# Trace of a matrix product: from casting loads on the software queue to plain float32 loads on SyncE's hardware queue, two rows to a partition

## The chip, the cores and the metric

The kernel runs on one core of a Trainium2 chip. The metric is device time in microseconds (us), lower is better. A run lasts some 740 us, and the spread of the kernel before is 0.03% (737.23 to 737.42 us).

The DMA figures are for the sixteen DMA engines that serve the core. "GB/s" in a slice of a profile counts the bytes written. A load that rounds float32 to bf16 on its way writes half of what it reads, so for such loads the rate of reading is twice the figure shown.

## The reference

```python
B, N = 8, 2176
a, b = randn(B, N, N), randn(B, N, N)          # float32
prod = np.matmul(a, b)
traces = np.diagonal(prod, axis1=1, axis2=2).sum(axis=-1)   # 8 numbers
```

The trace of A·B is the sum over all i and j of A[i,j]·B[j,i]. No matrix product is needed: transpose B, multiply with A element by element, and add up. Each number of A and B is used once, so 2 × 8 × 2176² × 4 bytes = 303 MB have to come from HBM, the memory that holds the inputs, and little is computed on them.

## The kernel before

A of one batch is 17 blocks of 128 rows, B too. All loads go through GpSimd's software queue and are rounded to bf16 on the way. TensorE transposes 128 × 128 blocks of B into PSUM, the memory that takes its results, and one VectorE instruction multiplies 512 columns with A and adds them up.

```python
KGW = 4
a_pool = tile_pool(bufs=2 * NT); b_pool = tile_pool(bufs=2 * KGW); psum_pool = tile_pool(bufs=7)
for bi in range(BATCH):
    for j_blk in range(NT):                        # all of A of this batch
        a_tile = a_pool.tile([P, N], bf16)
        nc.gpsimd.dma_start(out=a_tile, in_=a[bi, j_blk * P:(j_blk + 1) * P, :])
    for kg in range(N_KG):                         # groups of four blocks of B
        for kc in range(kc_lo, kc_hi):
            b_tile = b_pool.tile([P, N], bf16)
            nc.gpsimd.dma_start(out=b_tile, in_=b[bi, kc * P:(kc + 1) * P, :])
        for j_blk in range(NT):
            # up to 4 transposes of b_chunks[i][:, j_blk block] into psum_tile [P, 512] bf16
            # tensor_tensor_reduce(a_tiles[j_blk][:, kc_lo*P:kc_hi*P] * psum_tile) -> acc column
    # ... (sum of acc into one column per batch; at the end one small matmul sums the partitions)
```

Of the kernel before, what the change touches and what calls it, by code (L numbers as in the profile page):

```python
# [1 line left out]

# [6 lines left out]


@with_exitstack
def kernel(
    ctx: ExitStack,
    tc: tile.TileContext,
    a: bass.AP,
    b: bass.AP,
    out: bass.AP,
):
    nc = tc.nc  # L20
    P = 128
    BATCH, N, N2 = a.shape
    assert N == N2
    assert N % P == 0
    NT = N // P

    KGW = 4
    F = KGW * P
    N_KG = (NT + KGW - 1) // KGW

    dt = mybir.dt.bfloat16

    const = ctx.enter_context(tc.tile_pool(name="const", bufs=1))
    identity = const.tile([P, P], dt, tag="identity")
    make_identity(nc, identity)
    ones = const.tile([P, 1], mybir.dt.float32, tag="ones")
    nc.vector.memset(ones, 1.0)  # L37
    batch_accs = const.tile([P, BATCH], mybir.dt.float32, tag="batch_accs")
    result_tile = const.tile([P, BATCH], mybir.dt.float32, tag="result")

    a_pool = ctx.enter_context(tc.tile_pool(name="a_pool", bufs=2 * NT))
    b_pool = ctx.enter_context(tc.tile_pool(name="b_pool", bufs=2 * KGW))
    psum_pool = ctx.enter_context(tc.tile_pool(name="psum", bufs=7, space=bass.MemoryType.PSUM))
    psum_small = ctx.enter_context(tc.tile_pool(name="psum_small", bufs=1, space=bass.MemoryType.PSUM))
    scratch_pool = ctx.enter_context(tc.tile_pool(name="scratch", bufs=4))
    acc_pool = ctx.enter_context(tc.tile_pool(name="acc", bufs=2))

    for bi in range(BATCH):
        a_tiles = []
        for j_blk in range(NT):  # L50
            a_tile = a_pool.tile([P, N], dt, tag="a")
            nc.gpsimd.dma_start(out=a_tile, in_=a[bi, j_blk * P:(j_blk + 1) * P, :])  # L52
            a_tiles.append(a_tile)

        acc = acc_pool.tile([P, NT * N_KG], mybir.dt.float32, tag="acc")

        for kg in range(N_KG):
            kc_lo = kg * KGW
            kc_hi = min(kc_lo + KGW, NT)
            gw = kc_hi - kc_lo  # L60
            fw = gw * P

            b_chunks = []
            for kc in range(kc_lo, kc_hi):
                b_tile = b_pool.tile([P, N], dt, tag="b")
                nc.gpsimd.dma_start(out=b_tile, in_=b[bi, kc * P:(kc + 1) * P, :])  # L66
                b_chunks.append(b_tile)

            for j_blk in range(NT):
                psum_tile = psum_pool.tile([P, F], dt, tag="bT")  # L70
                for i, b_tile in enumerate(b_chunks):
                    nc.tensor.transpose(  # L72
                        psum_tile[:, i * P:(i + 1) * P],
                        b_tile[:, j_blk * P:(j_blk + 1) * P],
                        identity,
                    )
                scratch = scratch_pool.tile([P, F], dt, tag="scr")
                nc.vector.tensor_tensor_reduce(  # L78
                    out=scratch[:, :fw],
                    in0=a_tiles[j_blk][:, kc_lo * P:kc_hi * P],  # L80
                    in1=psum_tile[:, :fw],
                    scale=1.0,
                    scalar=0.0,
                    op0=mybir.AluOpType.mult,
                    op1=mybir.AluOpType.add,
                    accum_out=acc[:, j_blk * N_KG + kg: j_blk * N_KG + kg + 1],
                )

        nc.vector.reduce_sum(  # L89
            out=batch_accs[:, bi:bi + 1], in_=acc, axis=mybir.AxisListType.X  # L90
        )

    batch_psum = psum_small.tile([1, BATCH], mybir.dt.float32, tag="bp")
    nc.tensor.matmul(batch_psum, ones, batch_accs, start=True, stop=True)  # L94
    nc.vector.tensor_copy(out=result_tile[:1, :BATCH], in_=batch_psum)  # L95

    nc.sync.dma_start(
        out=out.rearrange("(a b) -> a b", a=1),
        in_=result_tile[:1, :BATCH],
    )  # L100


# [1 line left out]
_INS = ['a', 'b']  # L104
_OUTS = [((8,), 'float32')]


# [23 lines left out]
```

## Time and profile before

| | before |
|---|---|
| time, median | 737.3 us |
| read from HBM | 303 MB |
| read rate in full slices | 2 × 214 = 428 GB/s |
| VectorE / TensorE busy | 50% / 37% |
| after the chain's last wait for a load | 17 us |

These are lines of the page of before: busy time of the engines (PE is TensorE, PEld its weight loads, DVE VectorE, ACT ScalarE, POOL GpSimd), the GB/s moved in each of 40 slices of 18.4 us, the queue that all loads use, and the shares of the chain that ended last.

```profile
PE 271.7 (37%) x2314; PEld 217.7 (30%) x2314; DVE 364.8 (50%) x1370; POOL 144.4 (20%) x278
GB/s 175 213 214 215 213 215 213 214 214 214 214 213 214 214 214 214 213 214 213 214 214 213 214 213 214 214 213 215 213 214 214 213 214 214 214 214 213 161 209 29
q0 software_dynamic: 39168, 151.54, 102.2%
HBM read 303.04 MB, written 0.00 MB: 412 GB/s over the span
DMA 80%; issue 16%; POOL 1%; DVE 1%; PE 0%; POOLq 0%; DVEq 0%
```

The queue's packets took 102% of sixteen engines' span (overlapping packets count twice), every slice but the first and the last few stands at 213 to 215 GB/s, and no other engine is near its limit. The loads bound the kernel. The exceptions at the end are 161 and then 29.

The chain of waits of before, near its end (start in us, duration in us, what):

```profile
705.64 12.94 DMA b_tile<-in_b_dram
718.63 0.30 PE psum_tile L72
...
732.96 0.25 DVE batch_accs L89
733.25 0.21 PE batch_psum L94 x2
```

The last wait for a load ends at 718.6 us and the span at 735.6. In between VectorE works off what it could not start earlier, because a group of four blocks of B must have landed before the first of its reductions can run. That is the tail of 17 us. (The very last block of B lands at 721.2 us by the trace, 14.4 us before the end, but its turn comes after the others.)

These are two groups of the same profile, by line and shape: engine, operation, shapes, count, busy time and the mean ns of one.

```profile
L78 DVE CUSTOM_DVE_ANT_0 scratch<-a_tile,psum_tile 128x512 bf16<-128x512 bf16 x544 | 333.5, 682 | 364.3 <-PE psum_tile L72 364.1
L72 PE MATMUL psum_tile<-identity,b_tile 128*128 128x128 bf16 x2312 | 271.5, 286 | 460.3 <-DMA b_tile<-in_b_dram 434.1 <-DVE acc L78 22.4
```

Both engines' idle time is released by the engine before them, and in the end by the loads.

### The profile page before, as it was taken

The page shows a single profiled execution, that of the slowest core. Times are in us where ns is not written, and L with a number is a line of the kernel's source. Part 1 is how long each engine was busy: PE and PEld are TensorE (multiplying, and loading weights), DVE is VectorE, ACT ScalarE, POOL GpSimd, SP SyncE. Part 2 cuts the span into 40 slices and gives each one's busy share as a digit, 9 for nine tenths or more (in the row PEclk, how much of TensorE's full clock was granted, in tenths as well). Part 3 has the DMA queues.
Part 4 walks back from the last instruction along what each step waited for, and adds up shares of the span by engine and source line. Part 5 has one row for each costly group of instructions (what it writes and reads, how often), then busy time and mean ns, then how long its engine had stood idle before and what let it go on. Part 6 is the DMA issues. An engine that isn't in the chain of part 4 may idle for free.

```text
span 735.6 us, 7232 instructions
## 1 busy us (share of the span) xinstructions
PE 271.7 (37%) x2314; PEld 217.7 (30%) x2314; DVE 364.8 (50%) x1370; POOL 144.4 (20%) x278
## 2 busy tenths in 40 slices
PE   0016441174412744035450453505453054520665
PEld 0005430163301533024340343403342034410454
DVE  0007673087610967019570285704766056750698
POOL 4221221112121221212222122221222222221110
PEclk9999775557655556556655556555556556665575
DMA  8999999999999999999999999999999999999891
GB/s 175 213 214 215 213 215 213 214 214 214 214 213 214 214 214 214 213 214 213 214 214 213 214 213 214 214 213 215 213 214 214 213 214 214 214 214 213 161 209 29
DMA packets 39208, 152.00 MB, mean 207 GB/s; under 512 B 4354, under 2 KB 4354, under 8 KB 39170
## 3 DMA queue, kind: packets, MB, share of 16 engines
q0 software_dynamic: 39168, 151.54, 102.2%
q8 instruction: 18, 0.29, 0.1%
q14 instruction: 20, 0.16, 0.1%
q1 hardware_dynamic: 2, 0.00, 0.0%
HBM read 303.04 MB, written 0.00 MB: 412 GB/s over the span
## 4 chain that ended last, share of the span: by engine, by line
DMA 80%; issue 16%; POOL 1%; DVE 1%; PE 0%; POOLq 0%; DVEq 0%
DMA b_tile<-in_b_dram 51%; DMA a_tile<-in_a_dram 29%; POOL b_tile L66 1%; DVE scratch L78 1%; DVE acc L78 1%; POOL a_tile L52 0%; PE psum_tile L72 0%; POOLq L66 0%; POOL identity masks.py:199 0%; DVE batch_accs L89 0%; PE batch_psum L94 0%; DVEq L78 0%; POOL identity masks.py:197 0%; DVE result_tile L95 0%; POOLq masks.py:199 0%
## 5 line engine op out<-in xcount | busy, mean ns | idle before, releaser
L78 DVE CUSTOM_DVE_ANT_0 scratch<-a_tile,psum_tile 128x512 bf16<-128x512 bf16 (+1 forms) x680 | 362.3, 602 | 367.4 <-PE psum_tile L72 367.2
L72 PE MATMUL psum_tile<-identity,b_tile 128*128 128x128 bf16 x2312 | 271.5, 286 | 460.3 <-DMA b_tile<-in_b_dram 434.1
L72 PEld LDWEIGHTS <-b_tile 128*128 128x128 bf16 x2312 | 217.6, 132 | 513.8 <-DMA b_tile<-in_b_dram 465.6
L66 POOL DMA_DIRECT2D b_tile<-in_b_dram x136 | 71.8, 532 | 332.6 <-PE psum_tile L72 180.2
L52 POOL DMA_DIRECT2D a_tile<-in_a_dram x136 | 72.2, 533 | 238.0 <-DMA b_tile<-in_b_dram 112.4
L78 DVE DVE_READ_ACCUMULATOR2_ANT acc<- 128x1 f32 x680 | 55.9, 82 | 0.0
L89 DVE TENSOR_REDUCE batch_accs<-acc 128x1 f32<-128x85 f32 x8 | 1.9, 241 | 0.3
L94 PE MATMUL batch_psum<-batch_accs,ones 128*1 128x8 f32 x2 | 0.2, 173 | 1.5 <-DVE batch_accs L89 1.5
L94 PEld LDWEIGHTS batch_psum<-batch_accs,ones 128*1 128x1 f32 x2 | 0.1, 80 | 1.8 <-DVE batch_accs L89 1.8
L37 DVE MEMSET ones<- 128x1 f32 x1 | 0.1, 59 | 0.8 <-PEq L115 0.8
masks.py:199 POOL TENSOR_SCALAR_AFFINE_SELECT identity<-identity 128x128 bf16<-128x128 bf16 x1 | 0.3, 305 | 0.1
L95 DVE COPY result_tile<-batch_psum 1x8 f32<-1x8 f32 x1 | 0.2, 155 | 0.3 <-PE batch_psum L94 0.3
masks.py:197 POOL MEMSET identity<- 128x128 bf16 x1 | 0.2, 204 | 0.3 <-POOLq L115 0.3
L115 POOL MEMSET const-float32-0.0<- 128x1 f32 x1 | 0.1, 98 | 0.2 <-issue 0.2
L115 POOL MEMSET const-bfloat16-1.0<- 128x1 bf16 x1 | 0.1, 101 | 0.0
L115 POOL MEMSET const-uint8-127<- 128x1 uint8 x1 | 0.1, 101 | 0.0
L115 POOL MEMSET const-float32-1.0<- 128x1 f32 x1 | 0.1, 98 | 0.0
## 6 DMA issues: line engine op xcount, KB each, us to landing
a_tile<-in_a_dram POOLq DMA_DIRECT2D x136, 544.0 KB, 20.6
b_tile<-in_b_dram POOLq DMA_DIRECT2D x136, 544.0 KB, 20.3
out_dram<-result_tile SPq DMA_DIRECT2D x1, 0.0 KB
```

What stands on the lines that cost most here:

```text
L37: nc.vector.memset(ones, 1.0)
L52: nc.gpsimd.dma_start(out=a_tile, in_=a[bi, j_blk * P:(j_blk + 1) * P, :])
L66: nc.gpsimd.dma_start(out=b_tile, in_=b[bi, kc * P:(kc + 1) * P, :])
L72: nc.tensor.transpose(psum_tile[:, i * P:(i + 1) * P], b_tile[:, j_blk * P:(j_blk + 1) * P], identity,)
L78: nc.vector.tensor_tensor_reduce(out=scratch[:, :fw], in0=a_tiles[j_blk][:, kc_lo * P:kc_hi * P], in1=psum_tile[:, :fw], scale=1.0, scalar ...
L89: nc.vector.reduce_sum(out=batch_accs[:, bi:bi + 1], in_=acc, axis=mybir.AxisListType.X)
L94: nc.tensor.matmul(batch_psum, ones, batch_accs, start=True, stop=True)
L95: nc.vector.tensor_copy(out=result_tile[:1, :BATCH], in_=batch_psum)
L115: nc = _bacc.Bacc("TRN2", target_bir_lowering=False, num_devices=1)
```

## The change

The intent: use the hardware queue of SyncE, with large pieces (two rows of 8.7 KB lie side by side in HBM and go to one partition), and so relieve GpSimd. In this kernel the loads of that queue leave the numbers in float32, so ScalarE rounds A into a resident bf16 tile, and B stays float32 and is transposed so. A and B pass through the same ring of three staging buffers of 2.2 MB. The loop takes B by whole rows as they land, and splits the last two groups' loads into pieces for a short tail. The core of the diff, with cuts:

```diff
-            nc.gpsimd.dma_start(out=a_tile, in_=a[bi, j_blk * P:(j_blk + 1) * P, :])
-                nc.gpsimd.dma_start(out=b_tile, in_=b[bi, kc * P:(kc + 1) * P, :])
+    ROWS = 2
+    CHUNKS = [(0, 6), (6, 12), (12, NT)]
+    a_pool = ...(bufs=2)     # [P, 17, 2176] bf16 each
+    stage = ...(name="stage", bufs=3)
+    psum_pool = ...(bufs=3)  # [P, 6, P] float32 each
+    def load(src, start, m):                       # m rows to a partition: 2, or 1 for the odd last group
+        t = stage.tile([P, ROWS, N], f32, tag="stage")
+        rows = src[start:start + P * m, :].rearrange("(p r) k -> p r k", r=m)
+        nc.sync.dma_start(out=t[:, 0:m, :], in_=rows)
+    def load_a(a_all, bi, gi):
+        t = load(a[bi], start, m)
+        nc.scalar.copy(out=a_all[:, slot:slot + m, :], in_=t[:, 0:m, :])
     for bi in range(BATCH):
+        b_groups = row_groups(N, P, 1 if last else ROWS)
+        for gi, (start, m) in enumerate(b_groups):
+            b_tile = load(b[bi], start, m)         # last two groups of the run: in 4 pieces
+            if not last: load_a(a_next, bi + 1, gi)
+            for lo, hi in chunks:
+                for s in range(m):
+                    # 6 (or 5) float32 transposes into psum_tile, then one tensor_tensor_reduce
```

So the ring gets B, A, B, A, ...; A runs one batch ahead. In the last batch only B is left to load.

More of the change, by code (lines that the diff above doesn't have):

```diff
@@ L5, with row_groups @@
 import concourse.tile as tile
-from concourse import bass_utils, mybir
-from concourse import bass_isa
+from concourse import mybir
 from concourse.masks import make_identity
 from concourse._compat import with_exitstack
+def row_groups(n, p, rows):
+    groups, at = [], 0
+    while at < n:
+        m = min(rows, (n - at) // p)
+        groups.append((at, m))
+        at += m * p
+    return groups
 @with_exitstack
@@ L22 @@
     BATCH, N, N2 = a.shape
-    assert N == N2
-    assert N % P == 0
+    assert N == N2 and N % P == 0
     NT = N // P
-    KGW = 4
-    F = KGW * P
-    N_KG = (NT + KGW - 1) // KGW
+    ROWS = 2
+    CHUNKS = [(0, 6), (6, 12), (12, NT)]
+    LAST_CHUNKS = [(0, 6), (6, 12), (12, 16), (16, NT)]
     dt = mybir.dt.bfloat16
+    f32 = mybir.dt.float32
     const = ctx.enter_context(tc.tile_pool(name="const", bufs=1))
-    identity = const.tile([P, P], dt, tag="identity")
+    a_pool = ctx.enter_context(tc.tile_pool(name="a_pool", bufs=2))
@@ new lines @@
+    stage = ctx.enter_context(tc.tile_pool(name="stage", bufs=3))
+    psum_pool = ctx.enter_context(tc.tile_pool(name="psum", bufs=3, space=bass.MemoryType.PSUM))
+    psum_small = ctx.enter_context(tc.tile_pool(name="psum_small", bufs=1, space=bass.MemoryType.PSUM))
+    scratch_pool = ctx.enter_context(tc.tile_pool(name="scratch", bufs=2))
+    acc_pool = ctx.enter_context(tc.tile_pool(name="acc", bufs=2))
+    groups = row_groups(N, P, ROWS)
+    slot_cols = [(start + r, m) for start, m in groups for r in range(m)]
@@ new lines, in load @@
+    def load(src, start, m):
+        t = stage.tile([P, ROWS, N], f32, tag="stage")
+        rows = src[start:start + P * m, :].rearrange("(p r) k -> p r k", r=m)
+        nc.sync.dma_start(out=t[:, 0:m, :], in_=rows)
+        return t
+    def load_a(a_all, bi, gi):
+        start, m = groups[gi]
+        slot = start // P
+        t = load(a[bi], start, m)
+        nc.scalar.copy(out=a_all[:, slot:slot + m, :], in_=t[:, 0:m, :])
+    a_next = a_pool.tile([P, NT, N], dt, tag="a")
+    for gi in range(len(groups)):
+        load_a(a_next, 0, gi)
@@ L35 @@
+    identity = const.tile([P, P], f32, tag="identity")
     make_identity(nc, identity)
-    ones = const.tile([P, 1], mybir.dt.float32, tag="ones")
+    ones = const.tile([P, 1], f32, tag="ones")
     nc.vector.memset(ones, 1.0)
-    batch_accs = const.tile([P, BATCH], mybir.dt.float32, tag="batch_accs")
-    result_tile = const.tile([P, BATCH], mybir.dt.float32, tag="result")
-    a_pool = ctx.enter_context(tc.tile_pool(name="a_pool", bufs=2 * NT))
-    b_pool = ctx.enter_context(tc.tile_pool(name="b_pool", bufs=2 * KGW))
@@ L43 @@
-    psum_pool = ctx.enter_context(tc.tile_pool(name="psum", bufs=7, space=bass.MemoryType.PSUM))
-    psum_small = ctx.enter_context(tc.tile_pool(name="psum_small", bufs=1, space=bass.MemoryType.PSUM))
-    scratch_pool = ctx.enter_context(tc.tile_pool(name="scratch", bufs=4))
-    acc_pool = ctx.enter_context(tc.tile_pool(name="acc", bufs=2))
-    for bi in range(BATCH):
-        a_tiles = []
-        for j_blk in range(NT):
-            a_tile = a_pool.tile([P, N], dt, tag="a")
-            nc.gpsimd.dma_start(out=a_tile, in_=a[bi, j_blk * P:(j_blk + 1) * P, :])
-            a_tiles.append(a_tile)
-        acc = acc_pool.tile([P, NT * N_KG], mybir.dt.float32, tag="acc")
-        for kg in range(N_KG):
-            kc_lo = kg * KGW
-            kc_hi = min(kc_lo + KGW, NT)
-            gw = kc_hi - kc_lo
-            fw = gw * P
-            b_chunks = []
-            for kc in range(kc_lo, kc_hi):
-                b_tile = b_pool.tile([P, N], dt, tag="b")
-                nc.gpsimd.dma_start(out=b_tile, in_=b[bi, kc * P:(kc + 1) * P, :])
-                b_chunks.append(b_tile)
-            for j_blk in range(NT):
-                psum_tile = psum_pool.tile([P, F], dt, tag="bT")
-                for i, b_tile in enumerate(b_chunks):
-                    nc.tensor.transpose(
-                        psum_tile[:, i * P:(i + 1) * P],
-                        b_tile[:, j_blk * P:(j_blk + 1) * P],
-                        identity,
-                    )
-                scratch = scratch_pool.tile([P, F], dt, tag="scr")
-                nc.vector.tensor_tensor_reduce(
-                    out=scratch[:, :fw],
-                    in0=a_tiles[j_blk][:, kc_lo * P:kc_hi * P],
-                    in1=psum_tile[:, :fw],
-                    scale=1.0,
-                    scalar=0.0,
-                    op0=mybir.AluOpType.mult,
-                    op1=mybir.AluOpType.add,
-                    accum_out=acc[:, j_blk * N_KG + kg: j_blk * N_KG + kg + 1],
-                )
@@ new lines @@
+    batch_accs = const.tile([P, BATCH], f32, tag="batch_accs")
+    result_tile = const.tile([P, BATCH], f32, tag="result")
+    for bi in range(BATCH):
+        a_all = a_next
+        last = bi == BATCH - 1
+        b_groups = row_groups(N, P, 1 if last else ROWS)
+        acc = acc_pool.tile([P, NT * len(LAST_CHUNKS)], f32, tag="acc")
+        col = 0
+        if not last:
+            a_next = a_pool.tile([P, NT, N], dt, tag="a")
+        for gi, (start, m) in enumerate(b_groups):
+            pieces = last and gi >= len(b_groups) - 2
+            chunks = LAST_CHUNKS if pieces else CHUNKS
+            if pieces:
+                b_tile = stage.tile([P, ROWS, N], f32, tag="stage")
+                for lo, hi in chunks:
+                    nc.sync.dma_start(
+                        out=b_tile[:, 0, lo * P:hi * P],
+                        in_=b[bi, start:start + P, lo * P:hi * P],
+                    )
+            else:
+                b_tile = load(b[bi], start, m)
+            if not last:
+                load_a(a_next, bi + 1, gi)
+            for lo, hi in chunks:
+                for s in range(m):
+                    w = hi - lo
+                    psum_tile = psum_pool.tile([P, 6, P], f32, tag="bT")
+                    for u in range(lo, hi):
+                        c0, step = slot_cols[u]
+                        nc.tensor.transpose(
+                            psum_tile[:, u - lo, :],
+                            b_tile[:, s, c0:c0 + step * (P - 1) + 1:step],
+                            identity,
+                        )
+                    scratch = scratch_pool.tile([P, 6, P], dt, tag="scr")
+                    nc.vector.tensor_tensor_reduce(
+                        out=scratch[:, :w, :],
+                        in0=a_all[:, lo:hi, start + s:start + s + m * (P - 1) + 1:m],
+                        in1=psum_tile[:, :w, :],
+                        scale=1.0,
+                        scalar=0.0,
+                        op0=mybir.AluOpType.mult,
+                        op1=mybir.AluOpType.add,
+                        accum_out=acc[:, col:col + 1],
+                    )
+                    col += 1
@@ L89 @@
         nc.vector.reduce_sum(
-            out=batch_accs[:, bi:bi + 1], in_=acc, axis=mybir.AxisListType.X
+            out=batch_accs[:, bi:bi + 1], in_=acc[:, :col], axis=mybir.AxisListType.X
         )
-    batch_psum = psum_small.tile([1, BATCH], mybir.dt.float32, tag="bp")
+    batch_psum = psum_small.tile([1, BATCH], f32, tag="bp")
     nc.tensor.matmul(batch_psum, ones, batch_accs, start=True, stop=True)
```

## The prediction

> **What bounds the kernel now.** The loads. The page's queue part gives the software queue 102% of sixteen engines' span, and it reads 303.04 MB from HBM. The slices show 214 GB/s written nearly throughout; the loads halve the bytes (float32 in, bf16 out), so that is about 428 GB/s read. Every engine idles: the page has VectorE at 50%, TensorE at 37%. Two ends lie outside the stream. The chain of waits has the last load landing at 718.6 us, and the run ends at 735.6: a tail of 17 us, in which the last group of B is still worked off (68 reductions of 512 columns at 0.61 us, start to start, then 17 short ones). The windows view shows a dip too, to 166 GB/s, at 680 to 700 us, when the loads wait for B buffers. At full rate 303.04 MB take 708 us.
>
> **What changes.** The bytes read from HBM stay. The bytes written double, to 303 MB.
> - Rate of the loads: my estimate is 428 GB/s again (the same source rows, longer pieces), range 415 to 434. The Trainium skill, page "DMA: Bandwidth & Descriptors", section "Where 436 GB/s comes from", gives a ceiling of 435 GB/s; its table of streams issued from SyncE has 408.7. The trace of before (428) lies between.
> - GpSimd's 144 us of issuing go. They hid behind the stream: worth about nothing, apart from perhaps 1 us at the start.
> - VectorE: from the 682 ns (512 columns) and 283 ns (128 columns) of the groups by form, a column costs 1.04 ns. So 768 and 640 columns come every 0.87 and 0.74 us: 2.5 us for 128 rows of B, 338 us in all, hidden.
> - ScalarE: new. 4352 elements, [...]under the 5.2 us of one 2.2 MB load. Hidden.
> - TensorE: transposes now in float32. Bf16 ones came every 104 ns (61 in 6.33 us, half clock). The skill, "TensorE: Matmul & The Clock Gate", section "Terms", says transpose mode is four times faster for float32; I take that as one pass, about 107 ns. Before's trace can't show it. At 213 ns (two passes) only the last batch suffers; at 427 ns TensorE would bound the kernel at 987 us.
> - Three stage buffers: a B group is held for about 4.5 us after landing, an A group for about 4.5, with some 9 us before the queue would run dry. So no stall in the middle of a batch, perhaps 0.5 us at each batch's short last group.
> - In the last batch only B is loaded: 2.6 us for 128 rows against 2.5 us of VectorE, with three buffers. I expect 2 to 5 us lost there.
> - The tail: the last piece is 128 columns, so only some 3 us follow the last landing, in place of 17.
>
> **Sum.** Start 2.5, stream 708, stalls 3, tail 3: **716 us**, 0.971 of before; 8 in 10 between 703 and 738. Faster by over 2%: 0.6; within 2%: 0.29; slower: 0.11. So the gain is the shorter tail and steadier stream, not the hardware queue.
>
> **What would show it.** After: DMA at 9 in every slice, 420 to 432 GB/s; tail after the last load 3 to 4 us; float32 transposes every 105 to 130 ns; 768-column reductions 0.95 us; ScalarE's copies below 4.6 us; SyncE's queue waiting mostly for buffers of loads that have just landed, without a gap in the DMA row except in the last batch.
>
> **What would make it wrong.** A float32 stream near 409 GB/s, since twice the bytes enter SBUF: 741 us of stream alone. Transposes of several passes. Stage buffers freed late, so that two loads are not always queued. A hardware-queue stream at the ceiling (435) gives about 705.

## The result, and the profile after

The changed kernel takes 761.35 us (median of four runs, 759.14 to 763.47), against 737.26. The ratio is 1.033 (95% interval 1.030 to 1.035). A ratio here is the mean time of one kernel's fast runs over that of the other's of the same rounds, so it is not quite the ratio of the medians quoted. The change made the kernel slower by 3%. Variants with the same arithmetic (e1, e4) gave right results.

The same lines of the page of after (slices of 18.9 us; these loads write what they read, so the figures compare with 428):

```profile
PE 397.4 (52%) x2314; PEld 380.3 (50%) x2314; DVE 359.2 (47%) x830; ACT 261.6 (35%) x73; POOL 0.7 (0%) x6
GB/s 380 428 425 417 412 420 421 390 426 395 429 407 388 395 424 404 386 391 431 426 417 380 426 428 423 393 366 402 410 414 410 371 404 432 425 416 371 377 343 224
q1 hardware_dynamic: 22754, 303.05, 97.3%
HBM read 303.04 MB, written 0.00 MB: 400 GB/s over the span
DMA 67%; PE 19%; ACT 12%; issue 1%; DVE 0%
```

The bytes are the same and the second and third slices reach 428 and 425, but then the row is ragged, and it drops for the last four slices. TensorE and ScalarE, idle half of the time and more, have 31% of the chain between them. The row of DMA busy shares stands at 9 in all slices but the last all the same: a share of busy time did not show the gaps, and the GB/s did.

What SyncE's queue waited for before it could issue (us in total, times, longest):

```profile
SPq L55 <- PE psum_tile L105: 381.0, 75, 7.0
SPq L55 <- ACT a_next L62: 195.6, 72, 3.8
```

Each issue waits for a buffer, mostly one that TensorE holds. Such a wait alone need not cost anything: in the run of the loads alone (e3 below) the queue waits 648 us for buffers that are still being filled, and the stream never starves. The chain of waits of after, around 300 us (start, duration, what):

```profile
277.08 11.31 DMA t<-in_a_dram
288.39 0.02 issue
288.42 3.83 ACT a_next L62
292.24 0.02 issue
292.26 11.58 DMA t<-in_b_dram
303.84 0.14 issue
303.97 6.49 PE psum_tile L105 x34
310.46 0.02 issue
310.48 10.48 DMA t<-in_a_dram
```

This is one buffer's life, twice round the ring. A load is issued, lands after 10 to 12 us, its buffer is held (3.8 us by ScalarE's rounding, 6.5 us by TensorE's 34 transposes; this time is called the hold from here on), and only then can the load three places later be issued. At 428 GB/s a load of 2.2 MB takes 5.2 us, so a turn of the ring, three loads, has 15.6 us. That is what the first stage shows, in which only A is loaded: 13.21 to 28.82 to 44.43 us in the same chain. The turn of A above takes 15.2 us (277.08 to 292.26) and that of B 18.2 (292.26 to 310.48): 33.4 us for six loads, against 31.2.

Three groups of after, by line and shape, as shown of before:

```profile
L105 PE MATMUL psum_tile<-identity,t 128*128 128x128 f32 x2278 | 392.4, 350 | 355.5 <-DMA t<-in_b_dram 353.4 <-DVE acc L111 2.1
L62 ACT CAST a_next<-t 128x4352 bf16<-128x4352 f32 x64 | 244.4, 3819 | 418.3 <-DMA t<-in_a_dram 409.1 <-DVE acc L111 9.3
L111 DVE CUSTOM_DVE_ANT_0 scratch<-a_next,psum_tile 128x768 bf16<-128x768 bf16 x272 | 254.8, 953 | 394.6 <-PE psum_tile L105 392.0 <-issue 1.7
```

A float32 transpose has a mean of 350 ns where a bf16 one had 286. These means overlap, so the pace is better read from who waits for them. VectorE's reductions in the timeline of after, lines between left out (start, duration, engine, line, operation, and in brackets the idle time before it):

```profile
305.54 0.95 DVE L111 CUSTOM_DVE_ANT_0 scratch<-a_next,psum_tile 128x768 bf16<-128x768 bf16 x1 [4.11 <-PE psum_tile L105]
...
306.82 0.95 DVE L111 CUSTOM_DVE_ANT_0 scratch<-a_next,psum_tile 128x768 bf16<-128x768 bf16 x1 [0.32 <-PE psum_tile L105]
...
308.10 0.95 DVE L111 CUSTOM_DVE_ANT_0 scratch<-a_next,psum_tile 128x768 bf16<-128x768 bf16 x1 [0.32 <-PE psum_tile L105]
```

VectorE waits for TensorE at each step: six transposes take 1.28 us, 213 ns each, at a granted clock (the share of TensorE's full clock that it was given) of 0.50 (windows view, 304 to 307 us). A whole group of 34 takes 6.47 us, 190 ns each, since the clock rises within it (0.77 from 308 to 310.4 us). In the last batch, at a granted clock of 0.95 (705 to 740 us), 17 take 2.27 us, 133 ns each. Bf16 transposes came every 104 ns at half clock before. VectorE (0.95 us) and ScalarE (3.8 us, under the 4.6 forecast) are where the prediction put them.

### The profile page after: what moved, and what is told of

The parts are those of the page before. It is cut to its first block, busy times and chain, and to the rows that moved or that the text cites. A ratio compares the mean times of both kernels' runs of the same rounds, so it can differ in the third digit from the quotient of the medians.

```text
span 757.4 us, 6386 instructions
## 1 busy us (share of the span) xinstructions
PE 397.4 (52%) x2314; PEld 380.3 (50%) x2314; DVE 359.2 (47%) x830; ACT 261.6 (35%) x73; POOL 0.7 (0%) x6
## 4 chain that ended last, share of the span: by engine, by line
DMA 67%; PE 19%; ACT 12%; issue 1%; DVE 0%
DMA t<-in_b_dram 35%; DMA t<-in_a_dram 32%; PE psum_tile L105 19%; ACT a_next L62 12%; DVE acc L111 0%; DVE scratch L111 0%; DVE batch_accs L123 0%; PE batch_psum L128 0%; DVE result_tile L129 0%
## 5 line engine op out<-in xcount | busy, mean ns | idle before, releaser
L105 PE MATMUL psum_tile<-identity,t 128*128 128x128 f32 x2278 | 392.4, 350 | 355.5 <-DMA t<-in_b_dram 353.4
L105 PEld LDWEIGHTS psum_tile<-identity,t 128*128 128x128 f32 x2278 | 375.9, 214 | 371.8 <-issue 343.0
L111 DVE CUSTOM_DVE_ANT_0 scratch<-a_next,psum_tile 128x768 bf16<-128x768 bf16 (+1 forms) x410 | 355.7, 904 | 394.8 <-PE psum_tile L105 392.0
L62 ACT CAST a_next<-t 128x4352 bf16<-128x4352 f32 (+1 forms) x72 | 260.3, 3617 | 437.9 <-DMA t<-in_a_dram 428.6
L111 DVE DVE_READ_ACCUMULATOR2_ANT acc<- 128x1 f32 x410 | 34.0, 83 | 0.0
L105 PE MATMUL psum_tile<-identity,b_tile 128*128 128x128 f32 x34 | 5.0, 293 | 0.7 <-DVE acc L111 0.5
L105 PEld LDWEIGHTS psum_tile<-identity,b_tile 128*128 128x128 f32 x34 | 4.4, 204 | 1.2 <-DVE acc L111 1.1
L123 DVE TENSOR_REDUCE batch_accs<-acc 128x1 f32<-128x51 f32 (+1 forms) x8 | 1.7, 207 | 0.3
```

The lines of the kernel that those rows point to most:

```text
L62: nc.scalar.copy(out=a_all[:, slot:slot + m, :], in_=t[:, 0:m, :])
L105: nc.tensor.transpose(psum_tile[:, u - lo, :], b_tile[:, s, c0:c0 + step * (P - 1) + 1:step], identity,)
L111: nc.vector.tensor_tensor_reduce(out=scratch[:, :w, :], in0=a_all[:, lo:hi, start + s:start + s + m * (P - 1) + 1:m], in1=psum_tile[:, :w, :],
L123: nc.vector.reduce_sum(out=batch_accs[:, bi:bi + 1], in_=acc[:, :col], axis=mybir.AxisListType.X)
```

## The experiments

Theory 1: the stream itself can run at 428 GB/s, and it starves because staging buffers come back late, or hold too little. Theory 2: a plain float32 stream, with twice the bytes written, is slower. Theory 3: the traffic of the compute engines slows it. The queue itself is a fourth suspect. Kernels marked "wrong" leave out work to measure what remains. The diffs are shortened.

### e3_loads_only: nothing reads the loads

```diff
-        nc.scalar.copy(out=a_all[:, slot:slot + m, :], in_=t[:, 0:m, :])
-            for lo, hi in chunks:
+            for lo, hi in []:          # no transposes, no reductions
```

> All loads of the changed kernel, same order, same ring of three stage buffers, but nothing reads them (the result is wrong on purpose); a load then waits only for the landing of the load three before it. Theory 1 (the stream can run at 428 GB/s; after the change it starves because buffers come back late): steady 425 to 430 GB/s, 303 MB in about 708 us, 710 to 720 us in all. Theory 2 (a plain float32 stream, which writes twice the bytes into SBUF, is itself slower): again about 400 to 410 GB/s, 740 to 755 us.

Measured: 716.64 us (one look, wrong on purpose). Its GB/s row:

```profile
GB/s 374 430 427 428 430 427 431 424 430 426 432 426 427 430 427 431 425 429 426 432 426 428 428 427 431 425 431 424 431 427 429 429 425 432 425 430 424 421 422 343
```

Same loads, same ring, 428 GB/s flat. Theory 2 falls: twice the bytes written cost nothing. The change loses 44.7 us against its own loads (761.35 − 716.64). Only the last stretch, where rows go singly, stands at 421; that comes back below.

### e2_short_hold: a third of the work on each B group

```diff
-    CHUNKS = [(0, 6), (6, 12), (12, NT)]
+    CHUNKS = [(0, 6)]
```

> The changed kernel, but of each B group only the first chunk of six column blocks is transposed and reduced (wrong on purpose), so a B buffer is held about 2.5 us after landing, not 6.5. All loads and ScalarE's copies stay. Theory 1 (late buffers): the waits of SyncE's queue for TensorE shrink, the stream goes to 420 GB/s or more until the last batch, total 718 to 735 us. Theory 2 (stream slow by itself): within 1% of 761 us, about 755 or more. Theory 3 (SBUF traffic of ScalarE's rounding slows the loads): also near 755, since the rounding stays.

Measured: 741.88 us (one look, wrong on purpose), 19.5 less than the change, but above the 718 to 735 expected of theory 1. The hold is 2.8 us in its chain. In the windows view (stretch, us, busy times, clock, DMA share, GB/s at the end), the middle of a batch, the end of that batch, and the last batch:

```profile
290.00:311.00 21.00, 5.79 (x27) 4.89 (x25) 4.00 (x10) 7.63 (x2) 0.00 (x0) 0.50 1.00 427
311.00:331.00 20.00, 4.58 (x20) 3.59 (x18) 4.02 (x9) 6.19 (x3) 0.00 (x0) 0.50 0.93 380
696.00:734.00 38.00, 21.40 (x90) 16.70 (x89) 13.95 (x29) 0.00 (x0) 0.00 (x0) 0.52 0.94 353
```

The middle is mended. The end of each batch (380) and the last batch (353) are not. What these have in common: groups of one row, which fill a two-row buffer by half. With three buffers in the ring, half-empty buffers mean fewer bytes on order. ScalarE's rounding stays in full here, and the middle reaches 427, so theory 3 falls as far as ScalarE goes.

### e1_one_row: six buffers of one row in place of three of two

```diff
-    ROWS = 2
+    ROWS = 1
-    stage = ...(name="stage", bufs=3)
+    stage = ...(name="stage", bufs=6)
```

> One row to a partition and six stage buffers of half the size: the same SBUF, the same bytes, the same transposes and chunks, but a buffer comes back after 17 transposes, and in the last batch all six buffers count where before each of three was half empty. Theory 1 (late buffers): 425 GB/s or more in the middle, last batch without gaps; 722 to 738 us, clearly under the 761 of the change. Theory 2 (stream slow by itself): no gain, or worse, as pieces halve to 8.7 KB: 755 to 775 us.

The ring has the same bytes as in the change, in smaller units. Measured: 739.01 us (four runs, 738.98 to 739.08; ratio to before 1.002), right result. It is 22 us faster than the change with all its work, but it misses the expected 722 to 738 by a little. Its GB/s row is flat, with no dips at the batch ends and none in the last batch, at a lower level:

```profile
GB/s 369 421 421 421 421 420 420 419 421 421 422 418 418 423 421 420 420 420 422 420 421 419 421 421 420 419 420 421 423 419 419 418 421 420 416 415 421 421 418 133
```

Flat means that nothing starves. Level 420 in place of 428 is either the smaller pieces (8.7 KB in place of 17.4) or the engines' traffic.

### e10_loads_one_row: loads only, one row to a partition

```diff
 (e3_loads_only, with)
-    ROWS = 2      # and bufs=3
+    ROWS = 1      # and bufs=6
```

> Loads only again (wrong on purpose), but one row to a partition and six buffers, so pieces of 8.7 KB in place of 17.4 KB, with the same bytes in the ring. The one-row version with all its work ran at a flat 420 GB/s. If the piece size sets that: 421 GB/s here too, 303 MB in 720 us, 726 to 730 us in all. If the traffic of ScalarE, TensorE and VectorE sets it: 428 GB/s and about 716 us, as with two rows.

Measured: 727.01 us (one look, wrong on purpose).

```profile
GB/s 368 422 421 421 421 422 422 421 422 422 420 421 422 422 421 422 422 420 422 422 422 421 422 422 420 422 422 422 421 421 422 421 422 422 421 421 421 421 422 338
```

With nothing else running the rate is 421 to 422 again, so the piece size sets it, worth some 10 us of 717. The engines' traffic costs at most 1 or 2 GB/s more: theory 3 falls.

### e4_gpsimd_queue: the same loads from GpSimd

```diff
-        nc.sync.dma_start(out=t[:, 0:m, :], in_=rows)
+        nc.gpsimd.dma_start(out=t[:, 0:m, :], in_=rows)
```

> The changed kernel with its big loads issued from GpSimd (software queue), still plain float32; the last pieces stay on SyncE. Theory 1: the queue does not matter, about 757 to 770 us. If the hardware queue itself were the cause: near 735 us, with 425 GB/s or more.

Measured: 782.38 us (one look), right result. That is 21 us slower than the change and outside both expectations. The hardware queue is not the cause of the loss; in this ring it is the better of the two. The chain has 17.9% "issue" (1.4% with SyncE), but that name misleads:

```profile
288.80 13.35 DMA t<-in_b_dram
302.16 0.02 issue
302.18 0.02 POOLq L55
302.20 6.64 issue
308.85 8.93 DMA t<-in_a_dram
```

In the timeline the 34 transposes of this group run from 302.29 to 308.55 us, and GpSimd issues the next load at 308.85: the 6.64 us are the hold again, and only the last 0.3 us are GpSimd's answer. An issue takes 528 ns there, and 330 on SyncE. By the landing times (worked out as under e12) 18 of the 21 us lie in the middle of batches, where gaps of 16 us become 34; why was not found.

### e5_a_cast_dma: half of the change

```diff
-        t = load(a[bi], start, m)
-        nc.scalar.copy(out=a_all[:, slot:slot + m, :], in_=t[:, 0:m, :])
+        nc.gpsimd.dma_start(out=a_all[:, slot:slot + m, :], in_=rows)   # rounds on the way, no staging
```

> Half of the change: A goes back to GpSimd's queue and is rounded on the way into its resident tile (no staging, no ScalarE); B stays plain float32 from SyncE with its ring of three, and with the same float32 transposes. Theory 1 (late buffers): the ring now turns once in two loads' time of B, 31 us, so it can't starve in the middle: 425 GB/s or more read up to the last batch, which keeps its gaps; 724 to 740 us. If float32 transposes cost time by themselves rather than by holding buffers: no change, near 757 to 761 us.

Measured: 730.57 us (one look), right result, 0.9% under before. The float32 transposes are all there (TensorE 395.7 us busy, 397.4 in the change) and 31 us are gone. The transposes cost time only through the buffers that they hold: B alone has the ring of three, so a turn has twice the time.

### e13_middle_hold: two thirds of the work

```diff
-    CHUNKS = [(0, 6), (6, 12), (12, NT)]
+    CHUNKS = [(0, 6), (6, 12)]
```

> The changed kernel with the first two of three chunks of each B group (24 of 34 transposes a group, wrong on purpose), so a B buffer is held some 4.7 us, between the 2.8 of the short hold (741.9 us) and the 6.5 of the change (761.4). If a buffer may stay away up to some 6 us before the stream notices (a threshold): 740 to 745 us. If every microsecond of hold costs its share: 750 to 753 us.

Measured: 740.99 us (one look, wrong on purpose). Two lines of its chain, the hold of a B buffer and the load that waited for it:

```profile
298.79 4.28 PE psum_tile L105 x24
...
303.09 11.18 DMA t<-in_a_dram
```

And its GB/s row:

```profile
GB/s 374 426 430 426 430 426 425 382 434 422 428 419 377 430 426 428 424 371 429 430 427 412 389 429 423 427 400 399 430 426 426 411 400 427 430 428 376 386 389 243
```

A hold of 4.3 us costs no more than one of 2.8 (741.0 against 741.9 us), and one of 6.5 costs 20 us. So the cost does not grow with every microsecond of hold: it sets in between 4.3 and 6.5 us. (These kernels also leave VectorE less work; the next but two, e11, has a short hold with all the work.) The dips at every fifth slice are the batch ends, again untouched.

### e9_small_buffer: no buffer half empty for B

```diff
+    small = ...(name="small", bufs=1)              # one row; acc shrunk to make room
     def load(...):
+        if src_is_b and m == 1: t = small.tile([P, 1, N], f32, tag="small")
-        b_groups = row_groups(N, P, 1 if last else ROWS)
+        b_groups = row_groups(N, P, ROWS)
-            pieces = last and gi >= len(b_groups) - 2
+            pieces = last and gi == len(b_groups) - 1
```

> The change with one more stage buffer of one row for the odd group of B at each batch's end, and with groups of two rows in the last batch too, so no two-row buffer is used half empty (only A's odd group). Middle of a batch unchanged. Theory 1, in its fuller form (bytes queued are what counts; half-empty buffers make the dips at the batch ends and in the last batch): those dips mostly go, worth 10 to 18 us: 743 to 752 us. If the dips have another cause (the wait for the resident A tile): about 757 to 761.

Measured: 741.21 us (median of four runs, 738.33 to 747.29; ratio to before 1.008), right result: 20 us faster than the change, just past the hopeful end of what was expected. Its lowest slice before the last is 398, where the change had 343, and the last batch no longer sags, while the middle stays ragged:

```profile
GB/s 376 424 427 431 425 424 404 426 398 417 421 412 421 405 415 424 423 423 426 423 426 420 426 420 410 407 418 427 418 426 410 408 408 422 415 428 423 429 417 173
```

### e12_small_and_short: both at once

```diff
 (e9_small_buffer, with)
-    CHUNKS = [(0, 6), (6, 12), (12, NT)]
+    CHUNKS = [(0, 6)]
```

> The short hold (first chunk only, wrong on purpose) and the extra small buffer together. Apart they took 19.5 and about 20 us off the changed kernel. If they are two separate losses of one stream, they add up: 719 to 727 us, near the 716.6 of the loads alone. If they are the same loss seen twice: 735 to 742 us.

Measured: 723.63 us (four runs, 722.96 to 724.22, wrong). The sum of the two effects from the change would be 761.35 − 19.5 − 20.1 = 721.8. They add up: these are two separate losses. The landing times packed in the traces say the same. Take each landing minus the one before it, less the time of the data (5.2 us, or 2.6 for one row). In the change these gaps come to 16 us in the middle of batches, 14 at their ends (the one-row loads and the three after them) and 8 in the last batch. In e2 they are 4, 11 and 6, in e9 13, 2 and 1, and here 2, 0 and 0. The row of e12 is nearly that of the loads alone:

```profile
GB/s 372 429 426 427 427 428 431 424 425 430 426 430 424 430 425 427 429 426 429 426 431 421 428 430 430 423 425 432 426 426 430 422 430 429 427 431 422 430 428 182
```

### e11_act_rounds_b: a shorter hold with a right result

```diff
+                b_row = b_pool.tile([P, N], bf16); nc.scalar.copy(out=b_row, in_=b_tile[:, s, :])
-                            b_tile[:, s, c0:...:step],      # float32 transposes
+                            b_row[:, c0:...:step],          # bf16 transposes, bf16 PSUM
```

> The change, but ScalarE rounds B too, row by row, into two bf16 rows, and B is transposed in bf16: a right result with a shorter hold, about 4.2 us (two copies of 2.0 us) in place of 6.5. Half-empty buffers stay. Theory 1: the middle of a batch runs at 425 GB/s or more, 738 to 748 us in all. If it were ScalarE's or the plain loads' traffic that slows the stream: 757 us or more, since ScalarE now does twice the work.

Measured: 745.38 us (four runs, 743.21 to 748.34; ratio to before 1.012), right result. B's buffer now goes back after two copies of 2.0 us, and the middle of a batch mostly runs at 423 to 430 GB/s, though ScalarE is busy for 528.0 us, twice as long:

```profile
GB/s 376 429 423 428 430 424 430 366 428 426 429 424 385 430 425 428 423 383 427 427 428 420 383 429 427 428 398 405 426 429 425 378 412 426 428 427 377 388 394 204
```

The dips at the batch ends and in the last batch remain. Once more a shorter hold buys 16 us, and more ScalarE traffic doesn't hurt.

### e7_both_cast: a version that beats both

The loads of before (GpSimd, rounded on the way, bf16 transposes) in the loop of after.

```diff
 (the changed kernel, with)
+    b_pool = ...(name="b_pool", bufs=5)            # [P, 2, N] bf16
+    nc.gpsimd.dma_start(out=b_tile / a_all slice, in_=rows)     # both cast, no staging, no ScalarE
-    psum_pool = ...(bufs=3)   # float32
+    psum_pool = ...(bufs=6)   # bf16
     # A's loads of the next batch are issued one group later
```

> A version meant to beat both: the loads of before (GpSimd's queue, rounded on the way, bf16 transposes) in the loop of after (whole rows of B, worked off as they land, last ones in pieces), five bf16 buffers of two rows for B and A's loads one group later. Theory 1: 428 GB/s read throughout, and a tail of some 5 us in place of 17: 716 to 726 us. If the tail of before was not what made it 29 us longer than its stream: no better than 732.

Measured: 720.30 us (four runs, 720.17 to 720.36; ratio to before 0.977, interval 0.9755 to 0.9784), right result. Its GB/s row, to be doubled for the reads:

```profile
GB/s 175 216 215 215 216 216 213 217 216 216 216 215 217 215 216 215 215 216 216 215 215 217 215 216 215 215 215 217 215 215 217 213 218 216 215 216 213 214 214 98
```

And the end of its chain of waits:

```profile
696.55 10.70 DMA t<-in_b_dram
707.30 0.83 PE psum_tile L113 x6
...
716.19 0.21 PE batch_psum L136 x2
```

Between the first and the last slice none is below 213, so the dip near the end is gone, and the chain's last wait for a load is followed by 11 us in place of 17 (from the last landing, 5.2 in place of 14.4). So some 6 to 9 of the 17 us gained are the tail; the rest is the dip and a level of 215 to 216 in place of 214, not separated further. It is 41 us faster than the change: the loop of after was good, its staging was not.

## Why the prediction was wrong

The prediction was 716 us (703 to 738), and the result is 761.35.

- **Rate of the stream: right.** 428 GB/s was predicted, and the loads alone ran at 428. The alternative named as the first danger (409, from the Trainium skill's table of streams in "DMA: Bandwidth & Descriptors", section "iDMA fabric — 4 AXI ports for 8 engines, asymmetric across TPBs") did not come: that table has 4 KiB rows, these have 17.4 KB. No run here has 4 KiB rows, so whether the rows make the difference is not shown.
- **VectorE and ScalarE: right in size.** 0.95 us for 768 columns and 3.8 us for a copy. Neither engine bounds the kernel, though the copy is part of each turn of the ring.
- **Float32 transposes: wrong by a factor of two.** The step was "I take that as one pass, about 107 ns", from the skill's "4× faster for FP32" ("TensorE: Matmul & The Clock Gate", section "Terms"). Measured: 213 ns at a granted clock of 0.50 and 133 ns at 0.95. That set B's hold at 6.5 us in place of the 4.5 predicted. The prediction said that at 213 ns "only the last batch suffers". The middle suffered as well.
- **The step that failed: "Three stage buffers ... some 9 us before the queue would run dry. So no stall in the middle of a batch."** The right account of a buffer takes the whole turn. The very first load of after, with nothing ahead of it, took 8.61 us from issue to its landing, 3.4 more than its 5.2 us of data. So my estimate, worked out from these two numbers, is that a buffer may be away for 2 × 5.2 − 3.4 = 7.0 us, not 9, and only if all goes evenly. Holds of 2.8 and 4.3 us cost no more than each other, and 6.5 us costs about 20 us in all (e2, e13). How 6.5 can already cost, below the estimated 7.0, is seen in the landing times packed in the traces: loads do not come evenly. In the middle of batches the change's loads of A, which go into buffers that TensorE gave back, were issued 4.5 us (median) before the load ahead of them had landed; in e13 this margin was 5.3 us and in e2 7.4. In six runs together (the change, e2, e9, e11, e12, e13), loads with a margin under 4 us landed more than 0.2 us late in 12 cases of 19, from 4 to 5 us in 15 of 54, from 5 to 6 in 3 of 37, and over 6 in 12 of 306 (loads of two rows whose landing, and that of the load ahead, the traces hold). So the limit is not sharp: a longer hold eats the margin that would cover an uneven load. What makes loads uneven is not known.
- **The other half of the same step: "perhaps 0.5 us at each batch's short last group" and "2 to 5 us" in the last batch.** A one-row group fills a two-row buffer by half, so at the batch ends and throughout the last batch fewer bytes were on order. Avoiding that for B gave 20 us (e9; 14 to 23 over its runs). The prediction had noticed three buffers and one-row loads in the same sentence, and did not multiply them.
- **Sum of stalls: 3 us predicted, about 40 measured** (19.5 + 20.1 apart, 37.7 together in e12). The remaining 7 us between e12 and the loads alone lie mostly at the end, where e12 still works off what has landed: e12's last slice stands at 182 where that of the loads alone has 343.
- **Tail: "only some 3 us follow the last landing".** Too short. The last piece landed at 751.2 of 757.4 us, 6.2 us before the end, and the chain's last wait for a load ends at 745.5, because VectorE still had whole rows to work off while the small pieces landed.
- **"The gain is the shorter tail and steadier stream, not the hardware queue": the mechanism of the gain was right** and e7 shows it (0.977), but this kernel's ring took more than the loop gave.

Open: why a float32 transpose takes twice a bf16 one at half clock, what makes loads uneven, and why the stream starves more in e4.

## What to carry to other kernels

When loads bound a kernel, count how many bytes are on order at each moment: the buffers that wait for data, times their fill. A buffer drops out of this count from its landing until its reader gives it back, and a new load needs some time beyond that of its data (here 3.4 us for the first). A cast on the way cost nothing in this stream (428 GB/s read with it and without), halves the buffers and needs no staging at all, so giving it up for a "faster" queue has to pay for a ring of full-size buffers. Check a ring with a kernel that only loads, and look at GB/s in the slices rather than at the busy share of the DMA engines.

## What the Trainium skill lacked or had wrong

- "DMA: Bandwidth & Descriptors" has no rate of loads from HBM through SyncE's queue for pieces above 4 KiB (its 408.7 GB/s is for 4 KiB rows). Here it was 428 GB/s with 17.4 KB per partition and 421 to 422 with 8.7 KB.
- "DMA: Bandwidth & Descriptors", section "Anatomy of one DMA — SWDGE (gpsimd) path", puts the fixed cost of a DMA on GpSimd's path at about 2.0 us; the page gives no such fit for SyncE's. For the first load from SyncE, with two more queued behind it, 3.4 us lay on top of the 5.2 us that its bytes take at the full rate.
- "TensorE: Matmul & The Clock Gate" gives no time for a float32 transpose, only "4× faster for FP32". Here it was 213 ns at a granted clock of 0.50 and 133 ns at 0.95, against 104 ns in bf16 at half clock.
- The same page, section "Part 4: PE-mode transpose", says that the full clock does not engage for transposes. Here the clock granted in a stretch of nothing but transposes was 0.95 (705 to 740 us, float32), and a transpose took 133 ns there, against 213 at 0.50.
- No page says how many bytes a ring of staging buffers must have on order. Here three loads of 2.2 MB kept 428 GB/s with holds up to 4.3 us and not with 6.5.
